# Compressed branch of prompt attention: one batch per head pair, made one pair ahead, with some scalings and copies on GpSimd

## The chip, the cores and the metric

One core of one Trainium2 chip runs the kernel. The metric is the device time of one execution in microseconds (us); for several executions, their median. Engines in the profile: PE is TensorE's matrix product and PEld its weight load, DVE is VectorE, ACT ScalarE, POOL GpSimd, SP the engine that issues most DMAs.

## The reference

One inference step of a two-layer decoder trunk in fp32: 512 prompt tokens and 8 x 8 sample tokens, width 1024. The second layer's mixer is native sparse attention (NSA) with 12 query heads of 64, in 4 groups of 3 that share keys and values. For the prompt each head adds three branches, each weighed by a gate (with scores for selected and window keys taken over all causal keys, since 512 tokens are 8 blocks and 16 may be selected):

```python
s_c = einsum('btkgd,bnkd->btkgn', qg, ck) * ATT_SCALE - sl * dist_c      # 31 compressed blocks
p_c = softmax(where(dist_c >= 0, s_c, NEG_INF)) * any_c
o_c = einsum('btkgn,bnkd->btkgd', p_c, cv)
...
o = gg[..., 0:1] * o_c + gg[..., 1:2] * o_s + gg[..., 2:3] * o_w         # compressed, selected, window
```

## The kernel before

The kernel is one program in the Tile language: engines, tiles and waits are written as a sequence of calls, and a planner puts the instructions of each engine into one fixed order by an estimated timeline; on the chip each engine then takes its queue in that order. `_layer_b` projects (lines 1083 to 1127), makes keys and values (990 to 1044), compresses the prompt's keys and values (1047), runs memory attention, and then blends two generators: `_nsa_prompt` (1130) and `_nsa_sample` (1251), which yield rough durations so that `_blend` (508) can alternate them. After both comes the output projection, whose factors are differences of the attention's output (649) split into a high and a low part (185, 186).

`_nsa_prompt` works in 48 units: 2 key pairs `p`, 3 heads `g` of each group, 4 query tiles `qt` of 128 tokens, and `i` = 0 or 1. The two heads `s` of a pair are done together. `heads` (1135) loads the table of distances and slopes of each head (`tb`, 640 columns: 512 for keys, 4 x 32 for compressed blocks, in one buffer per head) and splits Q into a high and a low part, each copied into both halves of the partitions (1146 to 1149), in four buffers `v3`.

`scores` (1153) multiplies Q with the keys `KK` of the head, which hold 32 compressed, 512 selected and 512 window columns. For `i` = 0 it covers the compressed and selected columns together, in two PSUM tiles for the last query tile; for `i` = 1 the window. Then per region (compressed 32 columns, selected, window): VectorE adds the table and takes the minimum (1180), ScalarE takes the exponential with its sum (1187), VectorE the reciprocal (1190), GpSimd multiplies it with the gate (1191), and VectorE (1195) or in turn ScalarE (1197) scales the probabilities; the 32 columns always on VectorE.

`outputs` (1201) runs one unit behind: TensorE transposes each 128 columns of probabilities (190), with one more transpose for the 32 compressed columns; ScalarE and VectorE in turn copy up to four from PSUM into `pT` (1216, 1218); TensorE multiplies with the values (1225), the compressed ones being `cvp`, 32 partitions x 256. A product of two plain fp32 operands is recorded twice, one of rounded operands (`fp32r`) once. After `i` = 1 VectorE copies the sum into `Y` (1233).

## Time and profile before

| | us |
|---|---|
| median of three runs (1680.29 to 1683.44) | 1681.03 |
| the profiled execution | 1684.14 |
| its span from first to last instruction | 1682.4 |
| PE busy in the span | 1587.1 (94%) |
| DVE busy | 1257.1 (75%) |
| ACT busy | 794.6 (47%) |
| POOL busy | 663.8 (39%) |

The profile gives each instruction's start, duration, line and tile, and the wait that ended before it. Durations of products overlap, since they are pipelined: what a product costs in a row of products is the time from its start to the next one's. A line of the form `PEld pst L190 <- ACT sp L1187` says that the weight load of line 190 waited for ScalarE's work of line 1187 on tile `sp`; "issue" stands for time in which the engine waited for nothing that the profile shows.

### The profile page before, as it was taken

The numbers are of one execution on the slowest core, as the hardware profiler recorded it, in microseconds if no ns is written. First come the engines' busy times: TensorE is split into PE (matmuls) and PEld (weight loads), VectorE is DVE, ScalarE is ACT, GpSimd is POOL, SyncE is SP. The second block draws the span as 40 slices with busy tenths as digits, with TensorE's granted clock in tenths as the row PEclk, the third lists the DMA queues.
The fourth block names the chain that finished last, engine by engine and source line by source line (L and its number), as shares of the span: only waits on it lengthen the run. The fifth ranks groups of instructions, "written<-read, shape, count | busy, mean of one in ns | idle before, by whom it ended". The sixth has DMA issues, their size and how long they took to land.

```text
span 1682.4 us, 32056 instructions
## 1 busy us (share of the span) xinstructions
PE 1587.1 (94%) x11978; PEld 1469.8 (87%) x11978; DVE 1257.1 (75%) x2544; ACT 794.6 (47%) x1749; POOL 663.8 (39%) x682
## 2 busy tenths in 40 slices
PE   6999999998999999999999999999768999999996
PEld 6889999888999999998987867666668999999995
DVE  7664464649988888877455487776998888888886
ACT  5532242644434444444254387776455344444444
POOL 5001032218666655530000121212786756565541
PEclk9999999999999999999999999999798999999997
DMA  6512453352323223223254456552112232232212
GB/s 225 196 41 76 152 179 107 91 174 76 101 76 104 86 88 111 70 92 133 88 191 141 168 179 190 175 175 108 50 51 85 79 99 90 79 110 88 79 54 76
DMA packets 65061, 190.73 MB, mean 113 GB/s; under 512 B 9318, under 2 KB 16522, under 8 KB 54282
## 3 DMA queue, kind: packets, MB, share of 16 engines
q1 hardware_dynamic: 63560, 187.48, 33.7%
q8 instruction: 95, 1.56, 0.4%
q10 hardware_dynamic: 1346, 1.21, 0.3%
q14 instruction: 60, 0.49, 0.1%
HBM read 169.86 MB, written 18.80 MB: 112 GB/s over the span
## 4 chain that ended last, share of the span: by engine, by line
PE 80%; DVE 10%; issue 4%; DMA 2%; ACT 2%; SPq 1%; POOL 1%; DVEq 0%; ACTq 0%; POOLq 0%
PE psd L703 14%; PE pss L703 13%; PE psd L197 6%; PE psd L198 6%; PE psd L199 6%; PE pss L461 4%; PE pst L190 3%; PE pso L1225 3%; PE pst L199 3%; PE pst L197 3%; PE pst L198 3%; DVE wl L186 3%; PE pse L1354 2%; PE psd L1168 2%; PE pso L197 1%
## 5 line engine op out<-in xcount | busy, mean ns | idle before, releaser
L186 DVE TENSOR_TENSOR wl<-wq,wh 128x512 fp32r<-128x512 f32 x288 | 288.1, 1008 | 11.5 <-ACT wh L185 5.7
L197 PE MATMUL psd<-v,hi 128*128 128x288 f32 (+2 forms) x720 | 216.8, 302 | 15.1 <-ACT hi L185 11.3
L199 PE MATMUL psd<-v,lo 128*128 128x288 f32 (+2 forms) x720 | 214.7, 299 | 2.5 <-DVE lo L186 2.5
L198 PE MATMUL psd<-v,hi 128*128 128x288 f32 (+2 forms) x720 | 215.4, 300 | 0.2
L185 ACT ACTIVATE wh<-wq 128x512 fp32r<-128x512 f32 x288 | 174.5, 624 | 86.7 <-PE psd L703 26.0
L703 PE MATMUL psd<-oa,wh 128*128 128x288 f32 x672 | 143.8, 302 | 17.7 <-ACT wh L185 4.4
L197 PEld LDWEIGHTS psd<-v,hi 128*128 128x128 f32 (+1 forms) x720 | 136.8, 190 | 19.7 <-ACT hi L185 11.4
L703 PE MATMUL pss<-oa,wh 128*128 128x288 f32 x672 | 141.7, 299 | 10.0 <-DVE part L714 2.9
L703 PE MATMUL pss<-ob,wh 128*128 128x288 f32 x672 | 141.9, 299 | 5.2 <-DVE ob L186 5.2
L703 PE MATMUL psd<-ob,wh 128*128 128x288 f32 x672 | 141.6, 299 | 2.0 <-DVE ob L186 2.0
L199 PEld LDWEIGHTS psd<-v,lo 128*128 128x128 f32 (+1 forms) x720 | 136.9, 190 | 5.5 <-DVE lo L186 3.3
L198 PEld LDWEIGHTS psd<-v,hi 128*128 128x128 f32 (+1 forms) x720 | 137.3, 191 | 3.2 <-issue 1.6
L788 DVE TENSOR_TENSOR tmp<-part,tmp 128x288 f32<-128x288 f32 x88 | 88.6, 1006 | 54.7 <-POOL tmp L785 50.3
L783 POOL TENSOR_TENSOR tmp<-tmp,rs 128x288 f32<-128x288 f32 x88 | 96.0, 1091 | 84.5 <-DVE tmp L782 84.5
L703 PEld LDWEIGHTS psd<-oa,wh 128*128 128x128 f32 x672 | 109.7, 192 | 21.8 <-ACT wh L185 6.3
L703 PEld LDWEIGHTS pss<-oa,wh 128*128 128x128 f32 x672 | 108.8, 190 | 12.5 <-ACT v L678 2.5
L703 PEld LDWEIGHTS pss<-ob,wh 128*128 128x128 f32 x672 | 110.4, 192 | 5.9 <-DVE ob L186 5.9
L185 ACT ACTIVATE hi<-raw 128x1024 fp32r<-128x1024 f32 (+1 forms) x57 | 59.2, 1045 | 116.9 <-PE psd L198 108.9
L703 PEld LDWEIGHTS psd<-ob,wh 128*128 128x128 f32 x672 | 110.2, 192 | 2.4 <-DVE ob L186 2.4
L703 PE MATMUL psd<-oa,wl 128*128 128x288 f32 x336 | 101.7, 303 | 7.5 <-DVE wl L186 7.5
L703 PE MATMUL pss<-oa,wl 128*128 128x288 f32 x336 | 100.7, 300 | 2.4 <-DVE wl L186 2.4
L724 POOL TENSOR_TENSOR wq<-wq 128x512 f32<-128x512 f32 x48 | 68.1, 1420 | 87.5 <-DVE wl L186 87.3
(451 smaller groups left out, 4806.8 us busy)
## 6 DMA issues: line engine op xcount, KB each, us to landing
wq<-in_w_gu SPq DMA_DIRECT2D x44, 1024.0 KB
g<-in_cmp_pages SPq DMA_DIRECT2D x64, 256.0 KB
wd<-in_w_dn SPq DMA_DIRECT2D x32, 512.0 KB
raw<-in_w_in_a SPq DMA_DIRECT2D x9, 1024.0 KB
v<-in_cache_mem_kv SPq DMA_DIRECT2D x32, 256.0 KB
x<-in_slc_pages SPq DMA_DIRECT2D x32, 256.0 KB
raw<-in_slc_pages SPq DMA_DIRECT2D x32, 256.0 KB
wd<-in_w_dn SPq DMA_DIRECT2D x16, 384.0 KB
```

What stands on the lines that cost most here:

```text
L185: self.nc.scalar.activation(hi, src, AF.Copy)
L186: (eng or self.nc.vector).tensor_tensor(lo, src, hi.bitcast(F32), op=ALU.subtract)
L190: self.nc.tensor.transpose(out, in_, self.ident[:k, :k])
L197: nc.tensor.matmul(out, wh, xh, start=(k == 0), stop=False)
L198: nc.tensor.matmul(out, wh, xl, start=False, stop=False)
L199: nc.tensor.matmul(out, wl, xh, start=False, stop=(k == n - 1))
L461: nc.tensor.matmul(ps[:, :n], w[kv][i][:, lt, 2 * kp + k], x[j][:, k, lt:lt + n], start=(kp + k + lt + i + j == 0), stop=(kp == 3 and k + ...
L703: nc.tensor.matmul(ps, u[x][:, k // 2, k % 2], b[k // 2][y][:, k % 2], start=(k == 0 and x + y == 0), stop=(k == 3 and x == 1))
L724: nc.gpsimd.tensor_tensor(a11, a21, a11, op=ALU.subtract)
L783: nc.gpsimd.tensor_tensor(g, g, r, op=ALU.mult)
L788: nc.vector.tensor_tensor(g, out, g, op=ALU.mult)
L1225: nc.tensor.matmul(po()[64 * s:64 * s + 64, :P], v, w, start=(i + j == 0), stop=(i == 1 and j == len(todo) - 1))
```

## The change

The compressed branch leaves the 48 units. A new function `compressed` does it for both heads and all four query tiles of a pair at once: 16 products of 32 columns into one PSUM tile, an add of the tables and a maximum on VectorE, the subtraction on GpSimd, one exponential of 256 columns on ScalarE, sum and reciprocal on VectorE, gate and scaling on GpSimd, two transposes, and one copy to `CT`. A row range of `CT` (32 partitions for each query tile) is the operand of the output product, so `cvp` now holds the compressed values four times, once for each 32 partitions. `begin` makes Q's split, the tables and `CT` of the next pair after the third query tile of the pair before it; for this `tb` has two sets of buffers, Q's split alternates between `v3` and a new tile `qx`, and the scratch that the compiler keeps for DMAs shrinks to 256 bytes. `scores` now covers selected or window columns alone, takes the reciprocal and the gate of both heads together, and scales by VectorE, ScalarE, VectorE and GpSimd in turn. One copy of Q's low part moves from VectorE to GpSimd.

```diff
-    c.cvp = c.t("cvp", [32, 256], pool=pool)
+    c.cvp = c.t("cvp", [P, 256], pool=pool)
...
+            four = c.t("tmp")[:, :512]
+            nc.vector.tensor_copy(four.rearrange("p (h r n) -> p h r n", h=4, r=4),
+                                  hid.rearrange("p (h n) -> p h n", h=4).unsqueeze(2).broadcast_to([P, 4, 4, 32]))
             for h in range(4):
-                nc.tensor.matmul(ps[:32, 64 * h:64 * h + 64], hid[:, 32 * h:32 * h + 32], c.w2[:, 1],
+                nc.tensor.matmul(ps[:, 64 * h:64 * h + 64], four[:, P * h:P * h + P], c.w2[:, 1],
                                  start=True, stop=True)
...
-    scale, spread = itertools.cycle("va"), itertools.cycle("av")
+    scale, spread = itertools.cycle("vavp"), itertools.cycle("av")
...
+        tb = c.t("tb", [P, 2, 640], pool=pool, bufs=2)
...
+            nc.sync.dma_start(tb[:, s], io["ptab"][6 * p + 3 * s + g])
+            qh, ql = (c.t("v3", dt=F32R)[:, :NP_] if (p + g) % 2 else c.t("qx", [P, NP_], dt=F32R, pool=pool, bufs=4)
+                      for _ in range(2))
...
-            nc.vector.tensor_copy(ql[o:o + 64], ql[a:a + 64].bitcast(F32))
+            nc.gpsimd.tensor_copy(ql[o:o + 64], ql[a:a + 64].bitcast(F32))
...
+    def compressed(p, g, st, tb, out):
...
+        ss = c.psum("nq")
+        for s in range(2):
+            for qt in range(4):
+                for l in range(2):
+                    nc.tensor.matmul(ss[:, 128 * s + 32 * qt:128 * s + 32 * qt + 32], st[s][l][:, qt * P:(qt + 1) * P],
+                                     c.KK[2 * p + s][:, 0:32], start=(l == 0), stop=(l == 1))
+        C = c.t("cp", [P, 8, 32], pool=pool, bufs=2)
+        sm = c.t("cm", [P, 32], pool=pool, bufs=2)
+        m, d, r, cf = (sm[:, 8 * i:8 * i + 8] for i in range(4))
+        nc.vector.tensor_tensor(C.rearrange("p (s q) n -> p s (q n)", s=2),
+                                ss[:, :256].rearrange("p (s n) -> p s n", s=2), tb[:, :, 512:640], op=ALU.add)
+        nc.vector.tensor_reduce(out=m, in_=C, axis=AX.X, op=ALU.max)
+        yield 0.6
+        nc.gpsimd.tensor_tensor(C, C, m.unsqueeze(2).broadcast_to([P, 8, 32]), op=ALU.subtract)
+        nc.scalar.activation(C, C, AF.Exp)
+        nc.vector.tensor_reduce(out=d, in_=C, axis=AX.X, op=ALU.add)
+        nc.vector.reciprocal(r, d)
+        nc.gpsimd.tensor_tensor(cf.rearrange("p (s q) -> p s q", s=2), r.rearrange("p (s q) -> p s q", s=2),
+                                gates(p, g, slice(0, 4), 0), op=ALU.mult)
+        nc.gpsimd.tensor_tensor(C, C, cf.unsqueeze(2).broadcast_to([P, 8, 32]), op=ALU.mult)
+        yield 0.2
+        pt = c.psum("nt")
+        for s in range(2):
+            c.tr(pt[:, s * P:(s + 1) * P], C[:, 4 * s:4 * s + 4].rearrange("p q n -> p (q n)"))
+        nc.scalar.activation(out, pt[:, :2 * P], AF.Copy)
+        yield 0.2
...
-        regs = ((0, 32, 512 + 32 * qt), (32, 32 + n, 384 - P * qt)) if i == 0 else (
-            (544, 544 + n, 384 - P * qt),)
...
+        k0 = 32 + 512 * i
         for s in range(2):
...
+            ss = c.psum("nq")
+            w = max(n, 256)
+            for l in range(2):
+                nc.tensor.matmul(ss[:, :w], st[s][l][:, qt * P:(qt + 1) * P], c.KK[2 * p + s][:, k0:k0 + w],
+                                 start=(l == 0), stop=(l == 1))
...
+            nc.scalar.activation(S[:, :n], S[:, :n], AF.Exp, scale=-1.0, bias=m, accum_out=sm[:, o:o + 1])
             Ss.append(S)
...
+        cf = sm[:, 4 + 2 * i:6 + 2 * i]
+        nc.vector.reciprocal(cf, sm[:, 2 * i:2 * i + 2])
+        nc.gpsimd.tensor_tensor(cf, cf, gates(p, g, slice(qt, qt + 1), 1 + i)[:, :, 0], op=ALU.mult)
+        for s in range(2):
+            v, f = Ss[s][:, :n], cf[:, s:s + 1]
+            e = next(scale)
+            if e == "a":
+                nc.scalar.activation(v, v, AF.Copy, scale=f)
+            else:
+                (nc.vector if e == "v" else nc.gpsimd).tensor_scalar(out=v, in0=v, scalar1=f, scalar2=None,
+                                                                     op0=ALU.mult)
...
             if i == 0:
-                todo.append((S[:, 0:P], 32, c.cvp))
...
+                r = slice(32 * qt, 32 * qt + 32)
+                work[s].append((CT[r, s * P:(s + 1) * P], c.cvp[r, o:o + 64]))
...
+    def begin(p, g):
+        st, tb = heads(p, g)
+        CT = c.t("ct", [P, 2 * P], pool=pool, bufs=2)
+        yield from compressed(p, g, st, tb, CT)
+        ahead.append((st, tb, CT))
...
+            if qt == 2 and x < 5:
+                yield from begin(*pairs[x + 1])
...
-    nc = bacc.Bacc("TRN2", target_bir_lowering=False, num_devices=1)
+    nc = bacc.Bacc("TRN2", target_bir_lowering=False, num_devices=1, dynamic_dma_scratch_size=256)
```

## Rows read from the trace of the kernel before

**Rows 1.** Stage, us; busy: PE, PEld, DVE, ACT, POOL; clock, DMA, GB/s.

```profile
961.00:1173.00 212.00, 209.32 (x1796) 144.42 (x1794) 159.56 (x770) 158.09 (x479) 43.22 (x134) 1.00 0.54 171
```

**Rows 2.** Chain of waits in 961 to 1173 us, shares by line.

```profile
by line: PE pso L1225 22.3%; PE pst L190 19.6%; PE pse L1354 15.8%; PE psd L1168 15.6%; PE pss L1324 9.1%; PE pss L190 6.1%; DMA tb<-in_ptab 2.0%; DMA o_winv<-kvs 1.8%; PE pss L1331 1.1%; issue 0.9%; ACT sp L1187 0.6%; ACT v L1146 0.6%; ACT
```

**Rows 3.** Waits of weight loads, 961 to 1173; us, times, longest.

```profile
PEld pse L1354 <- issue: 12.5, 53, 0.4
...
PEld pst L190 <- ACT sp L1187: 1.5, 5, 0.8
...
PEld pss L1324 <- DMA x<-in_slc_pages: 0.2, 1, 0.2
```

**Rows 4.** Groups of TensorE in the stage, by shape; busy us, mean ns.

```profile
L1168 PE MATMUL psd<-kk,v 128*128 128x256 f32 x96 | 24.6, 327 | 0.9 <-DVE v L1149 0.8
...
L1168 PE MATMUL psd<-kk,v 128*128 128x512 f32 x24 | 8.5, 437 | 0.0
```

**Rows 5.** Timeline of TensorE; start us, duration, line, count.

```profile
1031.81 1.09 PE L190 MATMUL pst<-ident,sp 128*128 128x128 f32 x8
1032.66 0.75 PE L1168 MATMUL psd<-kk,v 128*128 128x256 f32 x4
1033.24 0.60 PE L190 MATMUL pss<-ident,hi 128*128 128x128 f32 x4
1033.77 1.08 PE L1324 MATMUL pss<-raw,v 128*64 128x512 f32 x4
```

**Rows 6.** Timeline of TensorE at the kernel's start.

```profile
25.91 2.39 PE L230 MATMUL pss<-ones,sq 128*128 128x1 f32 x20 [0.81 <-DVE sq L216]
28.16 0.38 PE L197 MATMUL pse<-v,hi 128*128 128x288 f32 x1
```

**Rows 7.** Timeline of TensorE, compressed values of the prompt.

```profile
869.82 0.63 PE L1078 MATMUL pse<-w,tmp 128*32 128x64 f32 x8
```

**Rows 8.** Groups of VectorE and ScalarE in the stage, by shape.

```profile
L1187 ACT ACTIVATION_READ_ACCUMULATOR sp<-sp,sm 128x1 f32 x144 | 27.4, 190 | 0.0
...
L1187 ACT ACTIVATE sp<-sp,sm 128x32 f32<-128x32 f32 x48 | 15.1, 315 | 11.2 <-DVE sm L1180 11.2
...
L1195 DVE TENSOR_SCALAR sp<-sp,sm 128x32 f32<-128x32 f32 x48 | 11.3, 235 | 3.6 <-POOL sm L1191 3.4
...
L1180 DVE CUSTOM_DVE_ANT_0 sp<-psd,tb 128x32 f32<-128x32 f32 x48 | 8.9, 185 | 5.5 <-PE psd L1168 2.8 <-DMA tb<-in_ptab 2.2
...
L1190 DVE RECIPROCAL sm<-sm 128x2 f32<-128x2 f32 x48 | 7.6, 159 | 2.7 <-ACT sp L1187 2.5
...
L1149 DVE CAST v<-v 64x512 fp32r<-64x512 f32 x10 | 4.7, 475 | 0.3
```

**Rows 9.** The same for ScalarE's scalings, all shapes together.

```profile
L1197 ACT ACTIVATE sp<-sp,sm 128x128 f32<-128x128 f32 (+3 forms) x48 | 26.6, 555 | 7.1 <-POOL sm L1191 6.9
```

**Rows 10.** Groups of GpSimd in the whole span, by shape.

```profile
L1393 POOL TENSOR_TENSOR hi<-v,dm 128x512 f32<-128x512 f32 x16 | 16.7, 1064 | 7.2 <-PE pss L190 5.4 <-DMA v<-in_tab 1.3 <-ACT sp L1187 0.5
...
L1509 POOL COPY v<-tmp 128x576 f32<-128x576 f32 x2 | 1.3, 670 | 13.6 <-PE psd L199 13.6
```

**Rows 11.** Chain of waits around two starts of a head pair.

```profile
1092.42 4.20 DMA tb<-in_ptab
...
1127.84 0.63 ACT v L1146
```

**Rows 12.** Timeline of VectorE behind the stage.

```profile
1173.49 0.74 DVE L649 TENSOR_TENSOR tf<-v 128x576 f32<-128x576 f32 x1
...
1177.86 1.82 DVE L649 TENSOR_TENSOR tf<-v 128x576 f32<-128x576 f32 x1
```

**Rows 13.** Timeline of GpSimd behind the stage.

```profile
1177.34 1.72 POOL L723 TENSOR_TENSOR wq<-wq 128x512 f32<-128x512 f32 x1
```

**Rows 14.** Waits of GpSimd, 961 to 1173 us.

```profile
POOL x L406 <- PE pse L1354: 17.4, 6, 4.3
POOL pn L1379 <- PE pss L190: 13.9, 6, 3.3
```

More of the change, by code (lines that the diff above doesn't have):

```diff
@@ L1201, in outputs @@
-    def outputs(p, qt, i, Ss, po):
+        k0 = 32 + 512 * i
+        for s in range(2):
+            ss = c.psum("nq")
[3 more added lines that the diff above has]
+                                 start=(l == 0), stop=(l == 1))
+            S = c.t("sp", pool=c.mb)
+            o = 2 * i + s
+            m = sm[:, 8 + o:9 + o]
+            nc.vector.tensor_tensor_reduce(
+                out=S[:, :n], in0=ss[:, :n], in1=tb[:, s, 384 - P * qt:384 - P * qt + n], scale=-1.0, scalar=3.0e38,
+                op0=ALU.add, op1=ALU.min, accum_out=m)
+            nc.scalar.activation(S[:, :n], S[:, :n], AF.Exp, scale=-1.0, bias=m, accum_out=sm[:, o:o + 1])
+            Ss.append(S)
+            yield 0.2 + 0.1 * qt
@@ L1219, in outputs @@
-            o = 64 * (2 * p + s)
-            work.append([(pT[:kn, j * P:(j + 1) * P], v[:kn, o:o + 64]) for j, (_, kn, v) in enumerate(todo)])
-            yield 0.11 * len(todo)
-        for j in range(len(todo)):
+            pT = c.t("pt", pool=c.mb)
+            pt = c.psum("nt")
+            m = qt + 1
+            for k in range(m):
+                c.tr(pt[:, k * P:(k + 1) * P], Ss[s][:, k * P:(k + 1) * P])
+            if next(spread) == "v":
+                nc.vector.tensor_copy(pT[:, :m * P], pt[:, :m * P])
+            else:
+                nc.scalar.activation(pT[:, :m * P], pt[:, :m * P], AF.Copy)
@@ L1223, in outputs @@
+            o = 64 * (2 * p + s)
+            work.append([(pT[:, k * P:(k + 1) * P], c.V[i][k // 2][:, k % 2, o:o + 64]) for k in range(m)])
+            if i == 0:
+                r = slice(32 * qt, 32 * qt + 32)
+                work[s].append((CT[r, s * P:(s + 1) * P], c.cvp[r, o:o + 64]))
+            yield 0.11 * m
+        n = len(work[0])
+        for j in range(n):
             for s in range(2):
                 w, v = work[s][j]
-                nc.tensor.matmul(po()[64 * s:64 * s + 64, :P], v, w, start=(i + j == 0),
-                                 stop=(i == 1 and j == len(todo) - 1))
@@ L1227, in outputs, with late @@
-        yield 0.27 * len(todo)
-    def late(p, g, qt, i, Ss, po):
-        yield from outputs(p, qt, i, Ss, po)
+                nc.tensor.matmul(po()[64 * s:64 * s + 64, :P], v, w, start=(i + j == 0), stop=(i == 1 and j == n - 1),
+                                 tile_position=(32 * qt if j > qt else 0, 64 * s))
+        yield 0.27 * n
+    def late(p, g, qt, i, Ss, po, CT):
+        yield from outputs(p, qt, i, Ss, po, CT)
         if i == 1:
@@ L1233, in late @@
             nc.vector.tensor_copy(y, po()[:, :P])
-    todo = []
-    units = [(p, g, qt, i) for p in range(2) for g in range(3) for qt in range(4) for i in range(2)]
-    for p, g, qt, i in units:
-        if qt == 0 and i == 0:
-            st, tb = heads(p, g)
-        if i == 0:
-            sm, po = c.t("sm"), _Lazy(lambda: c.psum("no"))
-        Ss = []
-        yield from scores(p, g, st, tb, qt, i, sm, Ss)
-        todo.append((p, g, qt, i, Ss, po))
-        if len(todo) > 1:
-            yield from late(*todo.pop(0))
+    def begin(p, g):
[3 more added lines that the diff above has]
+        ahead.append((st, tb, CT))
+    todo, ahead = [], []
+    pairs = [(p, g) for p in range(2) for g in range(3)]
+    yield from begin(*pairs[0])
+    for x, (p, g) in enumerate(pairs):
+        st, tb, CT = ahead.pop()
+        for qt in range(4):
+            for i in range(2):
+                if i == 0:
+                    sm, po = c.t("sm"), _Lazy(lambda: c.psum("no"))
+                Ss = []
+                yield from scores(p, g, st, tb, qt, i, sm, Ss)
+                todo.append((p, g, qt, i, Ss, po, CT))
+                if len(todo) > 1:
+                    yield from late(*todo.pop(0))
+            if qt == 2 and x < 5:
+                yield from begin(*pairs[x + 1])
     for a in todo:
```

62 lines of the change are left out of this document (5 added, 57 removed).

## The prediction

> **What bounds the kernel now.** I read the busy time of the engines in the stage that the diff touches first. It runs from 961 us, where the first score product of the prompt attention stands, to 1173 us, its last output product: 212 us of the 1682.4. Prompt attention is interleaved there with the sample attention (lines 1324 to 1429). TensorE is busy 209.3 of the 212 us, VectorE 159.6, ScalarE 158.1, GpSimd only 43.2, at the full granted clock of 2.4 GHz (1.00) [rows 1]. The chain of waits says the same: nearly all of it is TensorE's own lines, and the only prompt pieces off TensorE are the table loads (`tb`, 2.0%) and the splitting of Q (L1146) [rows 2]. Then I asked what TensorE's weight loads wait for. Most is "issue", which is TensorE's own order. The 40 other rows of the list, from 1.5 us down to 0.2 us, add to 17.7 us [rows 3]. So VectorE or ScalarE can give back at most those 17.7 us in this stage; at least 2.7 us is true idle time (212 - 209.3). After 1173 us comes a stretch set by VectorE that needs the last sample columns; the change doesn't touch its work.
>
> So the sum has to be made on TensorE first, although the diff mostly thins out VectorE and ScalarE.
>
> **Work on TensorE, part by part.** *Transposes.* Before there are 24 a head, 288 in all. The compressed block took one for each query tile and head (48); now it takes one for each head (12). So 36 go. Eight in a row take from 1031.81 to 1032.66, 0.106 us each [rows 5]: 36 x 0.106 = -3.8 us.
>
> *Narrower scores.* The 32 compressed columns leave the selected scores. Three of four query tiles get 32 columns narrower (288 to 256, 416 to 384, 544 to 512), in two products (high and low part) for 12 heads: 2304 columns. A column costs (437 - 327) / 256 = 0.43 ns [rows 4]: -1.0 us. The last tile also needs two products instead of four: 24 fewer. Four with 1088 columns took 0.58 us (1032.66 to 1033.24), of which the columns are 0.47, so 0.03 us each remains [rows 5]: -0.7 us. Together -1.7 (bounds -1.0, columns alone, and -4.5, if a product dropped saves all of its 0.145 us).
>
> *The new batch.* Each pair now issues 2 heads x 4 tiles x 2 parts = 16 products of 32 columns with a 128x128 weight load each: 96 in all. The trace has no such product with 32 columns. The nearest has one column behind a 128x128 load: 20 of them take from 25.91 to 28.16, 0.112 us each [rows 6], so the load sets the pace, not the columns. 96 x 0.112 = +10.8 us. Below this it can't come while each has its own load; the upper bound is the 0.145 us of the 256-column ones, +13.9. I take 10.8.
>
> *Changes of shape.* Between the last of four transposes and the next product with 64-wide weights there is 0.53 - 4 x 0.106 = 0.1 us lost [rows 5]. The batch adds one run of products and one of transposes a pair (12 x 0.1 = +1.2); the fifth transpose of the last tile had its own PSUM tile and copy for 12 heads, which goes (-1.2). Nothing net.
>
> *Compressed values* (`cvp`), now four times over the partitions: 8 records with 32-wide weights took 0.63 us [rows 7]; with 128-wide ones 8 x 0.112 = 0.9, and the VectorE copy of 512 columns in front, nearest the 512-column cast at 0.475 [rows 8], is waited for: +0.8 us (0 if other products fill it). The output products keep their number: 32 rows of `CT` in place of 32 rows of `pT`.
>
> Sum on TensorE: -3.8 - 1.7 + 10.8 + 0.8 = +6.1 us.
>
> **Work off TensorE.** VectorE loses 48 small adds (8.9 us), 48 reciprocals (7.6), 48 small scalings (11.3), the cast L1149 (12 x 0.475 = 5.7) [rows 8], and 60 accumulator reads and a few copies; it gains six batches of about 1.3 us. Some -30 to -35 us of 159.6. ScalarE loses 48 small exponentials (15.1) with their reads (48 x 0.19 = 9.1) [rows 8] and 24 of its 48 scalings (26.6 / 2 = 13.3) [rows 9], and gains six exponentials and six copies: about -35 us of 158.1. GpSimd gets 24 scalings, 12 copies and 18 batch operations, and 48 gate products instead of 96. One input of 576 columns takes 0.67 us there, two inputs of 512 columns 1.06 [rows 10]; so 24 x 0.5 + 12 x 0.6 + 6 x 1.4 - 10 = about +17 us on 43.2: still idle most of the time. All this is hidden under TensorE and costs nothing by itself; it is worth only what of the 17.7 us of waits it removes, and costs what new waits it makes.
>
> **What the earlier start of a pair removes.** `tb` and the split Q get a second set of buffers and are made during the third query tile of the pair before. On the chain now, one pair waits 4.2 us for `tb`, another for four splits of 0.63 us [rows 11]; TensorE has other work during most of it. Ahead move two loads on SP's queue and, for each pair, eight ScalarE splits, four VectorE ones and now four GpSimd copies. Queued behind a `tb` load that waits for the old tables are the page gathers of the sample attention, whose scores (L1324) wait for them; with two sets that wait goes, and the late transfer is hidden either way. The smaller DMA scratch only makes room; no load in the trace is issued by GpSimd, so nothing waits for it.
>
> I take 8 of the 17.7 us as removed, a little under half: the two engines lose a fifth of their work, and the waits at the start of a pair go. Bounds 2.7 (the true idle time) and 17.7.
>
> **Sum.** +6.1 - 8 = -2 us, against the profiled execution's own 1684.1 us (span 1682.4): 1682.1. That execution is 3.1 us above the median of 1681.0, so about 1679 us in the scale of the median. A change under 0.2% (3.4 us) can hardly be told from none here.
>
> **A rule weighed.** GpSimd and VectorE get in each other's way in this trace: a VectorE subtraction of 576 columns with two SBUF inputs takes 0.74 us where it starts ahead of GpSimd's, and 1.82 us where a GpSimd one is running [rows 12, 13]. The Trainium skill, "SBUF — State Buffer", section "Who interferes with whom", says that GpSimd shares one pair of ports with VectorE, that scalings and copies in VectorE's fast modes and operations with two SBUF inputs contend for it, and that the loser blocks for the whole instruction; the slowed rows agree. By that rule each of the moved operations can hold up a VectorE one by about its own length, so that VectorE would get back up to 12 + 7 + 8 = 27 us of its saving; with half of the 8 us of relief lost, the sum would be near +2 instead of -2, still inside the forecast's own range.
>
> **The rivals.** *1. The waits go altogether* (and runs on TensorE grow longer, because its operands are ready in order). For it: VectorE and ScalarE are both 75% busy and answer each other many times a unit. Against: 209.3 of 212 us busy. All 17.7 us go: 6.1 - 17.7 = -11.6, so about 1669.5 us. The Trainium skill, "Perfetto Trace Analysis", section "Identifying the Most-Contended Engine", would side with it: it judges TensorE by weight loads, not by busy products. Here loads are busy 144.4 of 212 us [rows 1], 68%, under VectorE's 75%, and by that rule VectorE's saving should show.
>
> *2. GpSimd's queue holds TensorE up: slower.* The batch passes VectorE, GpSimd, ScalarE, VectorE, GpSimd before its transposes: about 0.4 + 0.4 + 0.6 + 0.5 + 0.6 + 0.8 = 3.3 us without hops, taken between the rows of 32 and of 512 columns [rows 8, 10]. GpSimd takes its queue in order, and some entries there wait for the sample's products: L406 17.4 us in 6 waits, 4.3 at the longest, L1379 13.9 us [rows 14]. Behind such a wait now stand the batch, the copy of the split Q and the scalings. If the transposes come on TensorE less than about 4 us after the batch's scores, they wait, with all products behind them. At 1.5 us for each of 6 batches and 0.2 us for half of the 24 scalings: +11.4. With 6.1 - 8 that is +9.5, about 1690.5 us; it decides from some 5.5 us of such waits on (5.5 - 2 = +3.5).
>
> *3. Nothing is relieved.* The waits are covered by other products, and only the sum on TensorE stays: +6.1, about 1687 us. For it: the many short waits are each 0.2 us or little more, as long as a change of shape.
>
> **How the numbers follow.** Chances: forecast 0.38, rival 1 0.22, rival 2 0.25, rival 3 0.15. The forecast reaches from 1674 to 1684 (waits removed between 3 and 13 us), and holds faster 0.16, same 0.20, slower 0.02. Rival 1 is faster (0.21, with 0.01 same); rivals 2 and 3 are slower but for 0.07 where they come out small. Faster 0.37, same 0.28, slower 0.35. The range takes in most of rival 1 and rival 2: 1668 to 1691 us.
>
> **What would show it.** The stage from the first to the last score product should be 208 to 212 us. Right steps: 252 transposes in it, 96 small products at 0.11 us, VectorE and ScalarE 30 us and more less busy, no `tb` on the chain. Waits of transposes for GpSimd's scalings or for the batch would show rival 2; weight loads that hardly wait for ScalarE and VectorE, rival 1. The prediction is wrong if the planned order on TensorE gets more changes of shape, which no row of before can tell.

## The result, and the profile after

The change made the kernel slower: 1690.97 us median (1689.48 to 1692.72, 4 runs) against 1681.34 us (1680.29 to 1683.44, 4 runs) of the kernel before, ratio 1.0056 [1.0039, 1.0074]. Forecast were 1679.0 us and a range from 1668 to 1691, so the time lies in the range and on the wrong side of no change. The profiled execution took 1690.5 us (span 1688.7, granted clock 0.973; before 1684.1, 1682.4 and 0.975).

Where the 6.4 us between the two profiled spans arise, at landmarks that both kernels have (times from the start of the span):

| | before | after |
|---|---|---|
| last product of the first FFN | 748.2 | -0.7 |
| first evacuation of Q | 785.1 | +1.2 |
| stage's start (`kvs` ready) | 960.6 | +3.7 |
| first L703 product behind the stage | 1173.8 | +5.3 |
| 337th L703 product behind it | 1249.1 | +7.7 |
| end | 1682.4 | +6.4 |

So 3.7 us are there before the stage that the diff touches begins, and 4.0 come in the stage and behind it up to the 337th product; 1.3 are won back later. The stage of after, by busy time of the engines, in the form of [rows 1]:

```profile
964.30:1176.30 212.00, 208.03 (x1835) 146.99 (x1831) 145.88 (x560) 129.70 (x358) 71.43 (x133) 0.98 0.51 163
```

Beside [rows 1] TensorE is busy 1.3 us less of the same 212, VectorE 13.7 less, ScalarE 28.4 less, GpSimd 28.2 more. TensorE stays the bound. The chain of waits in the stage says so too; the table loads and most pieces of ScalarE, in the list of [rows 2], are gone from it, and the batch's products (L1166) and the wait for a store (`o_wink`) have come in:

```profile
by line: PE pso L1244 22.3%; PE pst L190 18.5%; PE pse L1383 16.0%; PE psd L1197 14.8%; PE pss L1353 9.8%; PE pss L190 6.7%; PE psd L1166 4.0%; DMA o_winv<-kvs 2.8%; DMA o_wink<-hi 2.0%; PE pss L1360 1.2%; issue 0.3%; ACT kvs L1036 0.2%; DV
```

What TensorE's weight loads wait for in the stage (us in total, times, longest). These are the first "issue" row, the longest single wait, and the largest rows that name another engine:

```profile
PEld pse L1383 <- issue: 14.5, 54, 0.8
...
PEld pss L190 <- issue: 3.3, 2, 3.1
...
PEld pss L190 <- DVE sm L1202: 1.6, 2, 0.8
...
PEld psd L1197 <- DVE pn L1368: 0.8, 1, 0.8
```

The rows that are not "issue" are 38 and add to 15.5 us, against 40 rows and 17.7 us in the same view of before [rows 3]. Two engines with 14 and 28 us less to do took only 2.2 us off the waits, and the 3.1 us in one piece are new, though they stand under "issue".

The stage itself, from `kvs` to the end of its last attention product, takes 213.2 us, against 212.8 before. So nearly all of the 4.0 us comes behind it, where VectorE's stretch (L649) begins at 1180.94 us instead of 1173.49 [rows 12]. In the planned order the sample attention's last product now ends at 1175.9 us, behind the prompt's; before, it ended at 1168.2. And three copies that L649 needs (L182) take 3.05 us instead of 0.93. VectorE and GpSimd there, after; then the same copies before:

```profile
1177.97 3.05 DVE L182 COPY v<-ys 128x64 f32<-128x64 f32 x3 [0.27 <-ACT ys L180]
...
1178.33 1.27 POOL L722 TENSOR_TENSOR s<-wq 128x512 f32<-128x512 f32 x1
...
1179.56 1.40 POOL L186 TENSOR_TENSOR oa<-v,oa 128x576 fp32r<-128x576 f32 x1
...
1180.94 3.87 DVE L649 TENSOR_TENSOR tf<-v 128x576 f32<-128x576 f32 x2
```

```profile
1172.64 0.93 DVE L182 COPY v<-ys 128x64 f32<-128x64 f32 x3 [0.27 <-ACT ys L180]
```

The batch on TensorE, in its timeline (start, duration, count):

```profile
1026.21 1.94 PE L1166 MATMUL psd<-kk,qx 128*128 128x32 f32 x16
1028.08 0.29 PE L1360 MATMUL pss<-KnT,v 128*64 128x8 f32 x4
```

16 products take from 1026.21 to 1028.08: 1.87 us or 0.117 each, the change of shape at their end included. Forecast were 0.112 and 0.1 for the change. The transposes are 252, as forecast (240 of `sp`, 12 of `cp`; groups by shape):

```profile
L190 PE MATMUL pst<-ident,sp 128*128 128x128 f32 x240 | 44.4, 290 | 0.0
...
L1166 PE MATMUL psd<-kk,v 128*128 128x32 f32 x48 | 5.8, 263 | 0.0
...
L190 PE MATMUL pst<-ident,cp 128*128 128x128 f32 x12 | 2.8, 320 | 0.0
```

The moved scalings, on GpSimd and on VectorE (groups, busy us and mean ns), beside [rows 8] and [rows 10]:

```profile
L1218 POOL TENSOR_SCALAR sp<-sp,sm 128x128 f32<-128x128 f32 (+3 forms) x24 | 28.3, 1178 | 2.2
```

```profile
L1218 DVE TENSOR_SCALAR sp<-sp,sm 128x512 f32<-128x512 f32 x12 | 7.0, 582 | 0.9 <-POOL sm L1211 0.9
...
L1218 DVE TENSOR_SCALAR sp<-sp,sm 128x384 f32<-128x384 f32 x12 | 5.4, 452 | 0.7 <-POOL sm L1211 0.6
...
L1218 DVE TENSOR_SCALAR sp<-sp,sm 128x256 f32<-128x256 f32 x12 | 4.4, 370 | 2.9 <-POOL sm L1211 2.9
...
L1218 DVE TENSOR_SCALAR sp<-sp,sm 128x128 f32<-128x128 f32 x12 | 3.9, 335 | 0.9 <-POOL sm L1211 0.9
```

A scaling on GpSimd takes 1.18 us on the mean, where 0.5 was taken, so GpSimd's busy time grew by 28 instead of 17 us. The same 48 scalings on VectorE took 20.7 us, 2.4 more than before (18.3; at 512 columns 582 ns instead of 480).

The longest new stall is at 977 us. All engines there, in order of start (the bracket is the idle time before, and who ended it):

```profile
975.63 0.20 POOL L1403 COPY hi<-KnT 128x16 f32<-128x16 f32 x1 [3.07 <-DMA o_wink<-hi]
975.78 0.20 POOL L1211 TENSOR_TENSOR sm<-sm,gq 128x2 f32<-128x2 f32 x1
...
976.01 0.45 DVE L1218 TENSOR_SCALAR sp<-sp,sm 128x256 f32<-128x256 f32 x1 [1.66 <-POOL sm L1211]
976.38 0.15 DVE L1366 RECIPROCAL ss<-ss 128x1 f32<-128x1 f32 x1
...
977.00 0.18 DVE L1368 TENSOR_SCALAR pn<-hi,ss 128x8 f32<-128x8 f32 x1
...
977.33 0.45 PE L190 MATMUL pss<-ident,pn 128*128 128x128 f32 x1 [2.81 <-DVE pn L1368]
```

Read it from the top. GpSimd's copy of the sample's new keys waits 3.07 us until a store has read its buffer. Queued behind it, the prompt's gate product (L1211) comes late; behind that VectorE's scaling waits 1.66 us; behind that the sample's small operations; and TensorE stands 2.81 us for `pn`. From 976.5 us, near the end of this stall, the granted clock is at the lower of its two levels for 6.8 us:

```profile
976.50:983.30 6.80, 5.50 (x22) 2.71 (x24) 2.30 (x13) 3.07 (x9) 1.47 (x6) 0.50 0.51 169
```

TensorE is busy for 5.5 us of these at half speed, so some 2.7 us are lost. So this looked like rival 2 at work, with about 5.5 us of price. The first part of the loss lies elsewhere: outside the touched code, at 787 us, TensorE waits for the evacuation of Q (L1095), where before its weight load waited 0.5 us. After (timeline), then before (waits):

```profile
786.78 0.32 PE L197 MATMUL psd<-v,hi 128*36 128x288 f32 x1 [2.59 <-DVE v L1095]
```

```profile
PEld psd L197 <- DVE v L1092: 0.5, 1, 0.5
```

### The profile page after: what moved, and what is told of

It is laid out like the page before. It is cut to its first block, busy times and chain, and to the rows that moved or that the text cites. A ratio compares the mean times of both kernels' runs of the same rounds, so it can differ in the third digit from the quotient of the medians.

```text
span 1688.7 us, 31769 instructions
## 1 busy us (share of the span) xinstructions
PE 1586.4 (94%) x12014; PEld 1475.3 (87%) x12014; DVE 1250.7 (74%) x2335; ACT 770.5 (46%) x1635; POOL 694.7 (41%) x688
## 4 chain that ended last, share of the span: by engine, by line
PE 80%; DVE 8%; issue 4%; POOL 3%; DMA 1%; ACT 1%; SPq 1%; DVEq 0%; ACTq 0%; POOLq 0%
PE psd L703 13%; PE pss L703 13%; PE psd L197 6%; PE psd L198 6%; PE psd L199 6%; PE pss L461 4%; PE pst L190 3%; PE pso L1244 3%; PE pst L199 3%; PE pst L198 3%; PE pst L197 3%; DVE wl L186 2%; PE pse L1383 2%; PE psd L1197 2%; PE pso L197 1%
## 5 line engine op out<-in xcount | busy, mean ns | idle before, releaser
L186 DVE TENSOR_TENSOR wl<-wq,wh 128x512 fp32r<-128x512 f32 x288 | 286.1, 1002 | 11.5 <-ACT wh L185 5.6
L703 PE MATMUL psd<-oa,wh 128*128 128x288 f32 x672 | 144.1, 302 | 21.9 <-DVE part L714 6.8
L703 PE MATMUL pss<-oa,wh 128*128 128x288 f32 x672 | 142.6, 301 | 8.4 <-DVE part L714 2.9
L703 PE MATMUL pss<-ob,wh 128*128 128x288 f32 x672 | 140.5, 297 | 4.9 <-DVE ob L186 4.9
L703 PE MATMUL psd<-ob,wh 128*128 128x288 f32 x672 | 141.5, 299 | 0.0
L703 PEld LDWEIGHTS psd<-oa,wh 128*128 128x128 f32 x672 | 109.8, 192 | 25.8 <-ACT wh L185 9.9
L703 PEld LDWEIGHTS pss<-oa,wh 128*128 128x128 f32 x672 | 109.9, 192 | 11.1 <-ACT wh L185 3.4
L703 PEld LDWEIGHTS pss<-ob,wh 128*128 128x128 f32 x672 | 109.5, 191 | 5.2 <-DVE ob L186 5.2
L703 PE MATMUL psd<-oa,wl 128*128 128x288 f32 x336 | 101.7, 303 | 12.7 <-DVE wl L186 12.7
L703 PEld LDWEIGHTS psd<-ob,wh 128*128 128x128 f32 x672 | 110.5, 193 | 0.0
L703 PE MATMUL pss<-oa,wl 128*128 128x288 f32 x336 | 100.8, 300 | 0.6 <-DVE wl L186 0.6
```

The lines of the kernel that those rows point to most:

```text
L186: (eng or self.nc.vector).tensor_tensor(lo, src, hi.bitcast(F32), op=ALU.subtract)
L703: nc.tensor.matmul(ps, u[x][:, k // 2, k % 2], b[k // 2][y][:, k % 2], start=(k == 0 and x + y == 0), stop=(k == 3 and x == 1))
```

## The experiments

All times are medians; the ratio is to the kernel before on the same chip, with its 95% interval. It is an estimate over all runs and differs from the quotient of the two medians by up to 0.1% (e1: 1.0011 by the medians). Differences between two variants are taken from their ratios. The changed kernel's own is 1.0056 [1.0039, 1.0074]. "Stretch" is the profiled time from `kvs` to the 337th L703 product behind the stage, 288.5 us before and 292.5 after. "Changes" are the places in the stage where TensorE goes from weights of one width (64 or 128 columns) to the other, counted in its timeline: 247 before, 207 after.

| | ratio | stretch | changes |
|---|---|---|---|
| e1 before, small scratch | 1.0016 [1.0006, 1.0027] | 286.2 | 245 |
| e2 after, no copy for `cvp` | 1.0052 [1.0039, 1.0065] | 294.6 | 207 |
| e3 after, key copy by DMA | 1.0038 [1.0026, 1.0051] | 289.3 | 207 |
| e4 after, half the batch's products | 1.0015 [1.0005, 1.0025] | 285.4 | 227 |
| e5 after, gate products on VectorE | 1.0059 [1.0047, 1.0071] | 291.9 | 237 |
| e6 after, no scalings on GpSimd | 1.0104 [1.0088, 1.0120] | 299.6 | 237 |
| e7 after, batch off GpSimd | 1.0110 [1.0094, 1.0126] | 296.9 | 245 |
| e8 before, small scratch, early start | 1.0039 [1.0026, 1.0052] | 289.7 | 243 |
| f1 before, GpSimd scalings | 1.0009 [1.0000, 1.0018] | 289.8 | 247 |
| f2 after, sample handed over sooner | 1.0059 [1.0047, 1.0072] | 291.9 | 221 |
| f3 before, sample handed over sooner | 1.0030 [1.0018, 1.0041] | 291.3 | 267 |
| f4 before, scratch 8192 | 1.0007 [0.9994, 1.0020] | 291.1 | 247 |
| g1 before, relief alone | 1.0002 [0.9990, 1.0014] | 288.2 | 241 |
| g2 after, not ahead | 1.0113 [1.0095, 1.0130] | 300.0 | 235 |

**e1, the scratch alone**

```diff
-    nc = bacc.Bacc("TRN2", target_bir_lowering=False, num_devices=1)
+    nc = bacc.Bacc("TRN2", target_bir_lowering=False, num_devices=1, dynamic_dma_scratch_size=256)
```

> The kernel before with the DMA scratch at 256 bytes and nothing else. Theory A (two waits of TensorE, 2.8 us on a sample transpose at 977 us and 0.9 us on the four-fold copy at 872 us, each with a fall of the granted clock to 1.2 GHz behind it, make the change slower): no difference from before, within 2 us of 1681.3. Theory B (the 96 small products make it slower by TensorE's work): the same, no difference. Theory C (the smaller scratch changes the planned order in the whole program, from the first stages on, and that costs time outside the attention): slower by 2 to 6 us, with the wait of 2.6 us at 787 us (L197 for VectorE's evacuation of Q) seen here too.

1684.76 us against 1682.95, ratio 1.0016: the edit that the prediction costed at nothing costs 2.7 us by the ratio (1.8 by the medians). The instructions are the same; in the trace TensorE's stand in another order from the 564th product on, at 93 us, and the wait at 787 us of the changed kernel is there:

```profile
785.39 0.45 PE L197 MATMUL psd<-v,hi 128*36 128x288 f32 x1 [2.59 <-DVE v L1092]
```

It stands, with 2.8 us on the weight load, in all eleven profiles with this scratch, and in none of the five with the default or with 8192 bytes (0.4 to 0.5 us there). The eleven reach the stage (`kvs` ready) at 961.5 to 969.3 us, the five at 958.0 to 961.6.

**e2, `cvp` without the copy in front**

```diff
-            four = c.t("tmp")[:, :512]
-            nc.vector.tensor_copy(four...)
-                nc.tensor.matmul(ps[:, 64 * h:64 * h + 64], four[:, P * h:P * h + P], c.w2[:, 1],
-                                 start=True, stop=True)
+                for r in range(4):
+                    nc.tensor.matmul(ps[32 * r:32 * r + 32, 64 * h:64 * h + 64], hid[:, 32 * h:32 * h + 32],
+                                     c.w2[:, 1], start=True, stop=True, tile_position=(0, 32 * r))
```

> The changed kernel, but the compressed values come four times over the partitions by 16 products into column groups of 32, without the VectorE copy in front. Theory A: the wait of 0.9 us at 872 us and the clock's fall for 3.4 us behind it go, 1 to 3 us less than the 1691.0 of the changed kernel. Theory B: no difference. Theory C: no difference.

1690.46 us, ratio 1.0052, not to be told from the changed kernel. TensorE's wait for the copy (0.86 us at 872 in the changed kernel) is gone, and at the same place it waits 1.79 us for another operand:

```profile
872.62 0.41 PE L197 MATMUL psd<-v,hi 128*128 128x288 f32 x1 [1.79 <-ACT hi L185]
```

**e3, the key copy by DMA.** The copy that waits in GpSimd's queue becomes a transfer on SP's queue.

```diff
-        nc.gpsimd.tensor_copy(wk[:, :, 512:], c.KnT[:, 1, :, 8 * b:8 * b + 8])
+        nc.sync.dma_start(wk[:, :, 512:], c.KnT[:, 1, :, 8 * b:8 * b + 8])
```

> The changed kernel, but the copy of the sample's new window keys, which holds GpSimd's queue for 3.1 us at 972.6 to 975.6 us while it waits for SP's queue, is done by a DMA. Theory A: GpSimd's gate products come on time, the 2.8 us wait of the sample transpose at 977 us goes and with it 6.8 us at 1.2 GHz: 4 to 7 us less than 1691.0. Theory B: no difference, since TensorE's work is the same. Theory C: no difference beyond a changed order, under 2 us.

1689.39 us, ratio 1.0038. The stall at 977 shrank from 2.81 us to 0.97, the low clock there from 6.8 to 3.4 us, and the stretch from 292.5 to 289.3:

```profile
976.57 0.30 PE L190 MATMUL pss<-ident,pn 128*128 128x128 f32 x1 [0.97 <-DVE pn L1368]
```

By the ratios that is 0.18% or 3 us below the changed kernel. The two intervals overlap: worked out from them, the gain lies between nothing and 6.6 us, so theory A's 4 to 7 us are not ruled out, but it isn't the whole loss.

**e4, half of the batch's products.** The compressed scores leave out the low part of Q: 48 products in place of 96.

```diff
-                for l in range(2):
-                    nc.tensor.matmul(ss[...], st[s][l][:, qt * P:(qt + 1) * P], c.KK[2 * p + s][:, 0:32],
-                                     start=(l == 0), stop=(l == 1))
+                nc.tensor.matmul(ss[...], st[s][0][:, qt * P:(qt + 1) * P], c.KK[2 * p + s][:, 0:32],
+                                 start=True, stop=True)
```

> The changed kernel, but the compressed scores leave out the low part of Q: 48 small products instead of 96. Theory B: 48 x 0.112 = 5.4 us less than 1691.0. Theory A: the products cost that only where TensorE is not waiting; with the waits kept, 2 to 5 us less. Theory C: the same as A.

1686.32 us, ratio 1.0015: 0.41% or 6.9 us below the changed kernel. By the two intervals the gain is 3.5 to 10 us. That fits theory B, 48 x 0.117 = 5.6 us, and it speaks for products that cost most of their price or all of it. It is no clean measure of it: the stall at 977 is 1.9 us shorter too, and the planned order has 20 more changes.

**e5, the gate products off GpSimd**

```diff
-        nc.gpsimd.tensor_tensor(cf, cf, gates(p, g, slice(qt, qt + 1), 1 + i)[:, :, 0], op=ALU.mult)
+        nc.vector.tensor_tensor(cf, cf, gates(p, g, slice(qt, qt + 1), 1 + i)[:, :, 0], op=ALU.mult)
```

> The kernel after, with the 48 gate products of the score units (a 128x2 multiply each) on VectorE instead of GpSimd; nothing else. Theory A (GpSimd's queue: the copy of the sample's new keys waits 3.07 us there for a store, the gate product behind it comes late, and behind that TensorE stands 2.81 + 0.48 us at 977 and then runs 6.8 us at the lower clock, some 3.4 us lost): the stall at 977 and the low clock behind it go, the time falls by 5 to 7 us against the kernel after, ratio to before about 1.002. Theory B (the price is TensorE's own work of the batch, and the stall is filled from elsewhere or comes back at another place): within 2 us of the kernel after, ratio 1.0045 to 1.006.

1692.70 us, ratio 1.0059. The mechanism of theory A was undone and the time was not: the long stall is 0.96 us, and the clock stays at its upper level (timeline, then the window 975 to 990):

```profile
977.88 0.30 PE L190 MATMUL pss<-ident,pn 128*128 128x128 f32 x1 [0.96 <-DVE pn L1368]
```

```profile
975.00:990.00 15.00, 14.01 (x123) 9.88 (x123) 10.98 (x46) 9.94 (x28) 4.84 (x9) 1.00 0.70 219
```

With the operations on other engines the planner orders TensorE differently inside the stage; changes of weight shape rise from 207 to 237, and TensorE loses some 8 us more at them (counted under "Changes of shape" below), more than the stall had cost. So the time came out as theory B said, but e5 can't decide on theory A. e3 is the better test of it, since it keeps the changed kernel's 207 changes: the held queue is real and worth some 3 us, not what alone separates the two kernels.

**e6, no scalings on GpSimd**

```diff
-    scale, spread = itertools.cycle("vavp"), itertools.cycle("av")
+    scale, spread = itertools.cycle("va"), itertools.cycle("av")
```

> The kernel after, with the scalings of the probabilities alternating between VectorE and ScalarE alone, as before the change; the 24 on GpSimd (0.65 us each, up to 1.08) are gone from its queue. If GpSimd's load of scalings is what makes it late (theory A in the form in which the prediction's rival had it): 3 us or more faster than the kernel after, ratio 1.003 or less. If it is the small gate product behind the waiting copy, whatever else the queue holds: the stall near 977 stays, within 2 us of the kernel after.

1698.39 us, ratio 1.0104, 8 us slower than the changed kernel: a miss for both. (The expectation's 0.65 us for a scaling on GpSimd is the price at 128 columns; the mean is 1.18.) The changes rise to 237 here too, with some 7 us more lost at them, and the clock is low for 3.4 us more in the stage (up to 1.7 us lost). Together that is about the 8 us.

**e7, the batch off GpSimd**

```diff
-        nc.gpsimd.tensor_tensor(C, C, m.unsqueeze(2)..., op=ALU.subtract)
+        nc.vector.tensor_tensor(C, C, m.unsqueeze(2)..., op=ALU.subtract)
...
-        nc.gpsimd.tensor_tensor(cf..., gates(p, g, slice(0, 4), 0), op=ALU.mult)
-        nc.gpsimd.tensor_tensor(C, C, cf.unsqueeze(2)..., op=ALU.mult)
+        nc.vector.tensor_tensor(cf..., gates(p, g, slice(0, 4), 0), op=ALU.mult)
+        nc.vector.tensor_tensor(C, C, cf.unsqueeze(2)..., op=ALU.mult)
```

> The kernel after, with the batch's three GpSimd operations (subtract, gate product, scaling; about 0.62 us each for the wide ones) on VectorE. The batch runs a pair ahead, so by the plan of the change it has some 8 us to spare; theory: no effect of its own, within 2 us of the kernel after, and the stall at 977 stays. Rival: the batch's way through GpSimd's queue is what is late at the pairs' starts, then 2 us or more faster.

1701.24 us, ratio 1.0110, 9 us slower than the changed kernel; again a miss for both. The stretch is 4.4 us longer, with 245 changes (+38, some 8 us more lost at them, and a shorter stall against it). Its profile was 4.6 us late already at the stage's start, though the planned order up to there is the changed kernel's: up to there the clock was low for 34 us, in the changed kernel's profile for 27.

**e8, the early start alone**

```diff
         if qt == 0 and i == 0:
-            st, tb = heads(p, g)
+            st, tb = ahead.pop()
...
+        if qt == 2 and i == 1 and (p, g) != (1, 2):
+            ahead.append(heads(*((p, g + 1) if g < 2 else (1, 0))))
```

with the second buffers for `tb` and the split Q, and the small scratch.

> The kernel before with the smaller scratch and with the tables and the split of Q made one pair ahead (second buffers for both), but with the compressed branch left in each unit as before, and nothing moved to GpSimd. Its base is the kernel with the smaller scratch alone (ratio 1.0016). Theory D (the relief of the pairs' starts, the 4.20 us for the table at 1092 among it, is real, and the batch spends more than it): 3 to 6 us faster than its base, ratio 0.998 to 1.000. Rival (the waits at the pairs' starts are only moved): within 1.5 us of its base, ratio 1.001 to 1.0025.

1690.12 us, ratio 1.0039, not faster but 0.23% slower than its base e1 (0.06 to 0.40% by the intervals). Theory D falls, and the rival's range is missed too: the 4.2 us for `tb` on the chain [rows 11] are not 4.2 us of time. In its profile the stage, from `kvs` to the last attention product, is 208.5 us, 4.3 shorter than before, and what follows up to the 337th L703 product is 81.2 us, 5.5 longer. What an early start gives inside the stage did not reach the end.

**f1, the GpSimd scalings alone**

```diff
-    scale, spread = itertools.cycle("va"), itertools.cycle("av")
+    scale, spread = itertools.cycle("vavp"), itertools.cycle("av")
...
-                if k1 - k0 == 32 or next(scale) == "v":
-                    nc.vector.tensor_scalar(...)
-                else:
+                e = "v" if k1 - k0 == 32 else next(scale)
+                if e == "a":
                     nc.scalar.activation(v, v, AF.Copy, scale=cf[:, r:r + 1])
+                else:
+                    (nc.vector if e == "v" else nc.gpsimd).tensor_scalar(...)
```

> The kernel before with one part of the change alone: a quarter of its scalings (12 on GpSimd in place of ScalarE's half, by the same cycle of four as the change has it). Scratch, buffers and batch stay as before. Taking the scalings off GpSimd made the changed kernel 8 us slower. Theory F (a scaling on GpSimd is a gain of its own, since VectorE and ScalarE come free for TensorE's next operands): 3 to 8 us faster than before, ratio 0.995 to 0.998. Rival (it was the planned order of TensorE that got worse there, with 237 changes of weight shape in the stage in place of 207; no gain of its own here): ratio 0.999 to 1.004, and changes of shape near the 247 of before.

1683.35 us against 1681.93, ratio 1.0009, with 247 changes as before. The rival is met. So e6 did not show that a scaling on GpSimd is worth something; theory F falls. (The expectation's "12 on GpSimd" is 24, a quarter of 96.)

**f2 and f3, the sample attention handed over sooner**, in the kernel after and in the kernel before.

```diff
-        _blend((nsa, 1.0), (sample, 2.0))
+        _blend((nsa, 1.0), (sample, 1.5))
```

> The kernel after, with the sample attention weighted 1.5 instead of 2.0 where the two attentions are blended: it is handed to the planner sooner, nothing else differs. Theory E (a part of the loss is the end of the sample attention, which comes at 1177 us in place of 1169.5 and leaves TensorE waiting 1.2 and 1.6 us alone there): first product behind the stage 3 to 6 us earlier, ratio 1.002 to 1.004. Rival (the end is set by the sum of TensorE's work, whatever the order): within 2 us of the kernel after, ratio 1.0045 to 1.007.

> The kernel before with the same weight of 1.5. Theory E would have little to give here (the sample's end at 1169.5 lies ahead of the prompt's at 1173): ratio 0.998 to 1.001. If it gains or loses more than 0.2% here as well, the planned order alone, at the same work, is worth as much as the change.

1692.76 us, ratio 1.0059: nothing for the kernel after, and the first product behind the stage came at 1186.9, later, not sooner. Theory E falls. In the kernel before the same number cost 0.30%, with 267 changes: at the same instructions, the planned order alone is worth half of what the change did.

**f4, half the scratch**

```diff
+    nc = bacc.Bacc("TRN2", target_bir_lowering=False, num_devices=1, dynamic_dma_scratch_size=8192)
```

> The kernel before with half of its scratch for DMA descriptors in place of a 64th (which gave 1.0016). Theory C (what costs is the other planned order that a differing layout gives, 108 lines of TensorE's plan instead of 516, not the scratch itself): ratio within 0.9990 and 1.0015, and the 2.6 us wait of TensorE for the evacuation of Q at 787 us comes or goes with the plan. Rival (the smaller scratch itself costs, evenly over the run): half of the 0.16%, and no single place where it arises.

1684.16 us, ratio 1.0007, too near to both for a verdict by the time. The profile has no 2.6 us wait at 787 us (it waits 0.4 there), which speaks for the order and not for the scratch as such.

**g1, the relief alone.** The small compressed operations of VectorE and ScalarE are left out, so that the compressed branch adds nothing, and TensorE keeps every product.

```diff
             for r, (k0, k1, t0) in enumerate(regs):
+                if k1 - k0 == 32:
+                    nc.gpsimd.memset(S[:, 0:32], 0.0)
+                    continue
...
             for r, (k0, k1, _) in enumerate(regs):
+                if k1 - k0 == 32:
+                    continue
```

> The kernel before with the small compressed operations left out and all of TensorE's work kept: in the 48 selected units of a head the 32 compressed columns get a GpSimd memset of zeros, in place of VectorE's add and scaling and ScalarE's exponential (the compressed branch then adds nothing to the output). VectorE loses some 20 us in the stage and ScalarE some 24, two thirds of what the change takes off them. Step of the prediction (8 of the 17.7 us of waits go with a fifth of the two engines' work): 3 to 6 us faster than before, ratio 0.9965 to 0.998. Rival (the waits don't hang on the load of the two engines but on the order of TensorE and on single chains; the relief is worth nothing): ratio 0.9985 to 1.0015.

1682.33 us against 1681.78, ratio 1.0002 [0.9990, 1.0014]. The stage, in the form of [rows 1]:

```profile
959.60:1171.60 212.00, 208.43 (x1801) 144.43 (x1798) 149.05 (x630) 146.40 (x387) 47.69 (x181) 1.00 0.53 171
```

VectorE is busy 10.5 us less, ScalarE 11.7 us less, TensorE the same within 0.9. The durations of the instructions left out add to some 22 us on each engine; the busy time falls by half of that, since instructions overlap on their engine. The waits that are not "issue" add to 21.9 us in 44 rows of this profile, against 17.7. The rival is met: by the interval at most 0.1% came back. The planned order is another one here as well (241 changes), so this holds as far as its order is not by chance a worse one; e1, f3 and f4, which alter no work, came out 0.07 to 0.30% slower.

**g2, the batch not ahead**

```diff
-    yield from begin(*pairs[0])
     for x, (p, g) in enumerate(pairs):
+        yield from begin(p, g)
         st, tb, CT = ahead.pop()
...
-            if qt == 2 and x < 5:
-                yield from begin(*pairs[x + 1])
```

> The kernel after, with each pair's batch (tables, split of Q, compressed scores and their softmax) at the pair's own start instead of a pair ahead; buffers and operations are the same. If the early start is worth what the prediction gave it (part of the 8 us, and cover for the 3.3 us of the batch's chain): 4 to 10 us slower than the kernel after, ratio 1.008 to 1.011. Rival (the early start by itself took 1.0016 to 1.0039 without the batch; it gives nothing, as TensorE has the sample's products there anyway): ratio 1.003 to 1.0065.

1701.82 us, ratio 1.0113, 0.57% or 10 us slower than the changed kernel (5 to 14 by the intervals): at the upper end of the first expectation, its ratio just above it. Why is not shown. The changes rise to 235, with some 9 us more lost at them, so the order alone can account for it. TensorE's transposes for the sample attention wait 7 times under "issue", 6.8 us in all; the longest, 3.2 us, is the stall of the changed kernel's 977 us:

```profile
PEld pss L190 <- issue: 6.8, 7, 3.2
```

## Why the prediction was wrong, step by step

**What bounds the stage: right.** TensorE stays busy 208 of 212 us, and dropping 48 small products (e4) gave time back. That the only prompt pieces off TensorE on the chain are `tb` and the split of Q is misread: the same line of [rows 2] has ScalarE's exponentials (L1187, 0.6%). And its sign, 208 to 212 us from the first to the last score product, fits the stretch to the last output product: to the last score product it is 202 us before and 197 after.

**The sum on TensorE, +6.1 us: right.** The products were 0.117 us each with their share of the change of shape (0.112 taken; not a floor, since the transposes with their own 128x128 loads take 0.106 [rows 5]), the transposes 252. I added up each product of the stretch at the pace of its columns or its load, whichever is longer: 194.7 us before and 200.2 after, +5.5. The forecast for the same part is 5.3 (the 0.8 for `cvp`, by its own terms 0.7, lies ahead of the stage).

**Changes of shape: mis-sized in the good direction.** Nothing net was forecast; they fell by 40. I added up what TensorE takes beyond that same pace at the places where the width changes, without those in the low clock and without waits above 0.6 us: 43.7 us at 244 places before, 35.3 us at 202 after. So a change costs some 0.18 us with the short waits that stand at it, not 0.1, and 8.4 us came back, more than the products cost. e5, e6, e7 and g2 have 229 to 241 such places again and 42.4 to 44.3 us at them. The transposes and products of these four are the changed kernel's; only their planned order is another.

**The work off TensorE: right in size, misread in worth.** By durations, the instructions of the stage took 30 us less on VectorE (206.7 to 176.9) and 41 less on ScalarE (194.4 to 153.1), where 30 to 35 and 35 were forecast. Busy time fell by 14 and 28 only, since durations overlap. GpSimd's scalings were taken as 0.5 us and took 1.18.

**The relief, -8 us: this step failed.** "I take 8 of the 17.7 us as removed, a little under half: the two engines lose a fifth of their work, and the waits at the start of a pair go." The waits came from 17.7 to 15.5 us, 2.2 less and not 8, and a new one of 2.81 with 6.8 us at the lower clock came in. g1 gave both engines relief at TensorE's full work and the time did not move (1.0002, at most 0.1% to the good by its interval). e8 took the waits at the pairs' starts and lost 0.23% to its base. My reading, which no run shows by itself: such a wait stands where the planned order lets TensorE meet the other engine, and free capacity there does not shorten it. How the number was chosen shows the fault too: "a little under half" rested on no row that a lighter engine shortens a wait.

**The scratch "only makes room": this step failed as well.** It changes no instruction, but the order: +2.7 us in e1 (interval 1.0 to 4.5).

**What follows the stage: this step failed too.** The prediction let the stretch behind the stage start when the sum says, since its work is untouched. The work is untouched, but its start moves: L649 comes 7.4 us later, 3.7 us because the stage begins later, the rest because the sample attention's last product and three copies ahead of it end later.

**The two together: near the measured time, in part by luck.** With the relief at nothing and 2.7 us for the scratch, the prediction's own sum is 6.1 + 2.7 = 8.8 us; measured were 9.6 (1690.97 - 1681.34). From e1 to the changed kernel it is 0.40%, 6.7 us. That is rival 3's time ("Nothing is relieved", 1687) with the scratch on top, but the profiles don't add up that way. In the stage the 5.5 us of products and some 7 us in the places of the stall and the low clock stand against 8.4 us less at the changes of shape and some 3 us less in other waits: 213.2 us against 212.8. What is lost lies ahead of the stage (3.7 us) and behind it.

**Rival 2 came out at the measured time (1690.5), and not for its reason.** GpSimd's queue did hold TensorE up once, by the way that it described (an entry that waits, the gate product behind it), but at the key copy and not at L406. e3 shortened this stall and won 0.18%, with an interval from nothing to 0.4%; e5 removed it and the low clock, and its other order took as much.

**The rule weighed** (the Trainium skill, "SBUF — State Buffer", section "Who interferes with whom") put up to 27 us of VectorE's saving at risk. In this trace VectorE's 48 scalings became 2.4 us longer beside GpSimd's (in e6, without those, they are 18.8 us by their durations, in the changed kernel 20.9), so in the stage contention is small. Behind the stage it is not: of the three copies of L182 one begins 0.02 us after GpSimd's L722 and one 0.02 us after its L186, and they take 1.31 and 1.44 us, as long as the GpSimd instructions; copies of this shape and line take 0.18 us where none begins ahead of them. That agrees with the rule, and it is some 2 us of L649's delay. The rule of the Trainium skill that rival 1 named ("Perfetto Trace Analysis", section "Identifying the Most-Contended Engine") would have had VectorE's saving show; g1 says that here it doesn't. The Trainium skill names there the share of the peak rate (MFU) beside the weight loads; the prediction took the loads alone.

**What stays open.** How the 9.6 us divide between the scratch's order, the stall and the order behind the stage: no run holds the order still while the work changes, and order alone moved the time by up to 0.30% (f3), perhaps by 0.5% (e6, e7, g2). The profiles differ by -2.6 to +4.1 us from before already at 371 us, where no variant differs from e1 or from before in its work. This goes with the granted clock of the execution: up to there it was low for 13.7 us in before and in e1, and for 23.9 us in e8, the latest. Eight profiles have the same order of TensorE up to the stage and reach it between 963.7 and 968.9 us, with 27 to 34 us at the lower clock. So a few us between two single profiles, at the stage's start, say little. No variant was faster than the kernel before.

## What to carry to other kernels

Before you credit a relief on engines that are not the bound, leave their work out and keep the bound's; one such run (g1) bounds the relief, and here it was 0.1% at most. Small products cost here 0.117 us each on the engine that bounds the stage, whatever they save elsewhere. Count the changes of weight width in the planned order as well: 40 of them were worth more here than 96 products less 36 transposes. Where a planner orders the queues, an edit that changes no work moved this kernel by 0.07 to 0.30%; a change of that size has to be held against such an edit, not against zero. And a stage that gets no longer can still end the program later, when what the next stage waits for comes last in it.

## What the runs showed that I had not expected

One stall of TensorE of 2.81 us came with 6.8 us at the lower clock (0.50), and a stall of 0.97 us at the same place (e3) with 3.4 us of it; with 0.94 us in e4 it was 6.8 us again, and with 0.96 us in e5 the clock stayed at 1.00. A VectorE copy of 64 columns took 1.31 us behind a GpSimd instruction that had begun 0.02 us before it, and 0.18 us without one. GpSimd scales 128 to 512 columns in 1.18 us on the mean where VectorE takes 0.43. The durations on VectorE and ScalarE overlap so far that 22 us fewer of them on each are only 10 to 12 us less busy time.
